# Layer 1's way out of attention: four K-tiles of the output weights converted during head 6, operand in two parts, sums begun between the last steps, last sums in small banks

## The chip, the core and the metric

The kernel runs on one core of a Trainium2 chip. The core has five engines with instruction streams of their own: TensorE (PE, matmuls and transposes; its weight loads are listed apart as PEld), VectorE (DVE), ScalarE (ACT), GpSimd (POOL) and SyncE (SP, which here only issues DMAs). An engine works through its stream in order and waits where an operand is not ready. Matmul results go into PSUM banks; all else lies in SBUF. The metric is device time of one launch in microseconds (us); lower is better.

## What is computed

Two layers over 512 latent tokens and 256 context tokens, width 1024, all in float32. Layer 1 is the one that matters here: eight heads of differential attention over all 768 keys, then an output projection, a gated residual, a norm and a SwiGLU block. Its context rows are needed as keys and values only, so its way out handles the 512 latent rows.

```python
def _diff_attend(q, k, v, lam):          # per head: two score maps
    s = einsum(q, k) * HEAD_DIM ** -0.5
    p = softmax(s)
    a = p[:, :, 0] - lam * p[:, :, 1]
    return einsum(a, v)
...
o = _rms(o, subln_w) * (1.0 - lam_init)          # per head
x = x + gx1 * (o.reshape(..., -1) @ w_out)       # way out of the mixer
x = x + gx2 * _swiglu(_rms(x, norm_ffn_w) * (1.0 + scx2) + shx2, ffn_w_in, ffn_w_out)
```

## The kernel before, in words

**Tiles.** Rows are taken in tiles of 128: latent tiles 0 to 3, context tiles 4 and 5. The contraction over the width runs in eight K-tiles of 128. Products keep float32 accuracy by splitting each operand into a high and a low part: three matmuls (hi·hi, hi·lo, lo·hi) per K-tile and per 512 output columns. A 1024 x 1024 product for one row tile is so 2 x 8 x 3 = 48 matmuls of 512 columns.

**Weights.** `unit` (L322) loads a raw tile by DMA on SP's queue, lets ACT cast it to the high part (L330) and lets DVE or POOL subtract to get the low part (L331). Raw tiles come from a ring of two (`raw_tile`), shared by all weights. `by_pieces` (L314) does the subtraction on POOL in pieces of 256 columns (L320). A high or low tile of a closed pool's place may be written once the tile that lay there is released.

**Layer 1.** For each head, `in_proj1` (L604) converts the head's weights with `by_pieces`, and then projects the six row tiles one by one (L428 to L430); each tile is normed and rotated (DVE, POOL), split, and transposed by the inner function `late()` (L647, L653), whose copies fill `qt` and `kT`. `attend1` (L659) is one step (head h, row tile t): scores into one of two wide PSUM slots (`p_sc`, L668 and L669), row maxima (L671), exponentials (L673), the difference of both maps (L680), then six transposes (`ppt`, L687), their copies (`PT`), the product with the values (`av`, L695), and a per-head norm (L697 to L702) that fills 128 columns of `o_t[t]`. `Staggered.push` puts the first half of a step ahead of the second half of the step before. All transposes take turns in two PSUM banks, `tr0` and `tr1` (`tr_tile`, L110): a new one waits until the tile two before it has been read.

**The way out of layer 1.** `OutProj` (L711): `weights` converts the eight K-tiles of `od_w_out`, `operand(t)` transposes `o_t[t]` into the room of the norm's output `hT` and splits it (L736 to L738), `sums(t)` makes both halves of 512 columns in one PSUM bank with a residual after each (L747 to L749, then L435 and L436), `last_sums` (L752) makes both halves at once in a wide slot. In the loop over head 7 (L1073 on), the weights begin at step 0, once the pools of the projection are closed (behind the marks of the last projected tile: `behind_marks`), K-tiles 0 to 3 in pool `w1u`, 4 to 7 in `w1d`. At steps 1 to 3 the loop adds `operand(t - 1)`, `sums(t - 1)` at a lower priority, and from step 2 the norm of tile t - 2. After the last step come `operand(3)`, the norm of tile 2, `last_sums(3)` and the norm of tile 3. The SwiGLU (`ffn`, L764) follows: for its first pair of hidden blocks it takes both wide slots and makes columns of rows 0 to 255 first (`first_segs`), then rows 256 to 511 (L791).

**Order.** The program is traced in the order of the source. A planner then lays out each engine's stream from priorities and its own model of time; the order on the chip is fixed. `tc.high_priority(-1000)` lowers the priority of what stands inside it, and `tc.issue_after(ins)` puts what stands inside it behind `ins` on the engine of `ins`. Turns in a tile ring follow the order of the source.

Of the kernel before, what the change touches and what calls it, by code (L numbers as in the profile page):

```python
# [63 lines left out]
def backbone(es: ExitStack, tc: tile.TileContext, x, c, ctx, c_ctx, mod_w, mod_b, norm_mix_w, norm_ffn_w,  # L64
# [50 lines left out]
    def f32(ap):  # L115
        return ap.bitcast(F32)
# [205 lines left out]
    def unit(pool, views, shape, bufs, name, sub=None, new_tile=raw_tile):  # L322

        raw = new_tile(shape, name + "r")
        for dst, src in views(raw):
            nc.sync.dma_start(dst, src)
        p_hi, p_lo = pool if isinstance(pool, tuple) else (pool, pool)
        hi = p_hi.tile(shape, F32R, name=name + "h", tag="whi", bufs=bufs)
        lo = p_lo.tile(shape, F32R, name=name + "l", tag="wlo", bufs=bufs)
        nc.scalar.copy(hi, raw)  # L330
        (sub or nc.vector.tensor_sub)(lo, raw, f32(hi))  # L331
        return hi, lo
# [271 lines left out]
    def in_proj1(h, tabs, wp, st, wh, qp):  # L604
# [14 lines left out]
        for t in CTX_FIRST:  # L619
# [35 lines left out]
            if t == CTX_FIRST[-1]:  # L655
                late()
# [48 lines left out]
    def out_units(wp, w_out, subs=(nc.gpsimd.tensor_sub,), rooms=(raw_tile,)):  # L705
        for k in range(KT):
            def views(raw, k=k):
                yield raw, w_out[0, k * P:(k + 1) * P, :]
            yield unit(wp[k // 4].pool, views, [P, D], 4, "wo", subs[k % len(subs)], rooms[k % len(rooms)])

    class OutProj:  # L711

        def __init__(self, l, units, o_t, xs, pool):
            self.l, self.units, self.ws, self.o_t, self.xs, self.g = l, units, [], o_t, xs, {}
            self.gates(2 if l == 0 else 1, pool, 0)
# [5 lines left out]
        def weights(self, n=KT):  # L721
            with behind_marks():
                self.ws.extend(w for _, w in zip(range(n), self.units))

        def operand(self, t):
            ohi, olo = tile_T(0, t), tile_T(1, t)
            if self.l == 0:
                self.xs[t] = load_x(t)
                nc.scalar.copy(ohi, self.o_t[t])
                nc.gpsimd.tensor_sub(olo, self.o_t[t], f32(ohi))  # L730
                return
            for q in range(2):
                pt = tr_tile("opt", [P, 4, P])
                for k in range(4):
                    kk = 4 * q + k
                    nc.tensor.transpose(pt[:, k, :], self.o_t[t][:, kk * P:(kk + 1) * P], ident)  # L736
                nc.scalar.copy(ohi[:, 4 * q:4 * q + 4], pt)
                nc.vector.tensor_sub(olo[:, 4 * q:4 * q + 4], pt, f32(ohi[:, 4 * q:4 * q + 4]))  # L738
            self.xs[t] = load_x(t, True)

        def sums(self, t, bank=None, pool=None, add=nc.vector):
            ohi, olo = tile_T(0, t), tile_T(1, t)
            for n in range(2):
                ps = acc_tile("ops", one=bank)
                for k in range(KT):
                    a, b = (z[:, n * 512:(n + 1) * 512] for z in self.ws[k])
                    nc.tensor.matmul(ps, ohi[:, k, :], a, start=k == 0, stop=False)  # L747
                    nc.tensor.matmul(ps, ohi[:, k, :], b, start=False, stop=False)  # L748
                    nc.tensor.matmul(ps, olo[:, k, :], a, start=False, stop=k == KT - 1)  # L749
                residual(self.xs[t], ps, self.g[0 if t < NTX else 1], n, pool, add, 1)  # L750
# [203 lines left out]
    for b in range(4):  # L954
# [9 lines left out]
        if b == 3:  # L964
# [7 lines left out]
            oproj = OutProj(0, out_units(ws, ev_w_out), o_t, xs, opa.pool)  # L972
# [72 lines left out]
    fp.close()  # L1045
    at = Pool("mix1")
# [60 lines left out]
    fp = Pool("ffn1")  # L1107
# [62 lines left out]
```

## Time and profile before

| | us |
|---|---|
| median of 3 runs | 1807.75 (1807.63 to 1808.97) |
| the profiled execution | 1810.42 |
| its span, first to last instruction | 1808.6 |
| mean granted TensorE clock | 0.985 |
| PE busy | 1725.4 (95%) |
| DVE, ACT, POOL busy | 1005.0, 809.2, 601.7 |
| last projection matmul of layer 1 begins | 1331.78 |
| first matmul of the way out begins | 1354.80 |
| first SwiGLU matmul of layer 1 begins | 1418.90 |
| first matmul of SwiGLU's second product begins | 1456.44 |

The page of the profile gives busy time per engine, a picture of the span in 40 slices with the granted clock, the chain that ended last and the costliest groups; its times count from the span's first instruction. Further views are the busy time by windows, the waits of an engine by the one that ended them, the groups by line and shape, and the timeline. In a windows row, "PE busy (xN)" is the time in which a matmul ran and the count of those that began; PEclk is 1.00 at full clock. In a group row the numbers after the bar are the summed busy time and the mean ns of one.

### The profile page before, as it was taken

The numbers are of one execution on the slowest core, as the hardware profiler recorded it, in microseconds if no ns is written. First come the engines' busy times: TensorE is split into PE (matmuls) and PEld (weight loads), VectorE is DVE, ScalarE is ACT, GpSimd is POOL, SyncE is SP. The second block draws the span as 40 slices with busy tenths as digits, with TensorE's granted clock in tenths as the row PEclk, the third lists the DMA queues.
The fourth block names the chain that finished last, engine by engine and source line by source line (L and its number), as shares of the span: only waits on it lengthen the run. The fifth ranks groups of instructions, "written<-read, shape, count | busy, mean of one in ns | idle before, by whom it ended". The sixth has DMA issues, their size and how long they took to land. (4 is left out here: it accounts for less than half of the span.)

```text
span 1808.6 us, 26168 instructions
## 1 busy us (share of the span) xinstructions
PE 1725.4 (95%) x9958; PEld 1462.3 (81%) x9958; DVE 1005.0 (56%) x1737; ACT 809.2 (45%) x1710; POOL 601.7 (33%) x866
## 2 busy tenths in 40 slices
PE   6999999989999999999999989999988899999998
PEld 3887776767888888888888889999986788888887
DVE  4776465444365555555543656665674455656553
ACT  6566555433354344344332566665663432222220
POOL 2753333321064344233312567776643100000000
PEclk8999999999999999999999999999989999999999
DMA  9212233213543234344421111111122233233231
GB/s 313 53 42 92 74 103 120 70 36 105 163 152 105 82 105 140 116 140 128 128 85 40 63 36 50 47 45 36 33 71 82 73 110 109 70 105 105 70 107 56
DMA packets 152477, 165.64 MB, mean 92 GB/s; under 512 B 16480, under 2 KB 139936, under 8 KB 152352
## 3 DMA queue, kind: packets, MB, share of 16 engines
q1 hardware_dynamic: 152000, 163.77, 28.7%
q8 instruction: 78, 1.28, 0.3%
q14 instruction: 47, 0.39, 0.1%
q10 hardware_dynamic: 352, 0.21, 0.0%
HBM read 159.73 MB, written 4.22 MB: 91 GB/s over the span
## 5 line engine op out<-in xcount | busy, mean ns | idle before, releaser
L435 DVE TENSOR_TENSOR dps<-dps,g 128x512 f32<-128x512 f32 x200 | 136.0, 695 | 108.5 <-PE dps L848 100.2
L846 PE MATMUL dps<-wdh,hdh 128*128 128x512 f32 x440 | 176.0, 401 | 0.9 <-DVE x L436 0.9
L847 PE MATMUL dps<-wdl,hdh 128*128 128x512 f32 x440 | 174.3, 396 | 0.0
L848 PE MATMUL dps<-wdh,hdl 128*128 128x512 f32 x440 | 168.1, 396 | 0.0
L428 PE MATMUL inps<-wih,hT 128*128 128x384 f32 x384 | 134.1, 349 | 2.3 <-ACT qkv L626 2.3
L436 DVE TENSOR_TENSOR x<-x,dps 128x512 f32<-128x512 f32 x200 | 131.9, 680 | 2.8
L429 PE MATMUL inps<-wil,hT 128*128 128x384 f32 x384 | 131.9, 343 | 0.0
L430 PE MATMUL inps<-wih,hT 128*128 128x384 f32 x384 | 131.4, 342 | 0.0
L791 PE MATMUL pg<-hT,wgh 128*128 128x512 f32 x352 | 129.8, 392 | 0.0
L791 PE MATMUL pu<-hT,wuh 128*128 128x512 f32 x352 | 129.4, 391 | 0.3 <-DVE x L436 0.3
L212 ACT ACTIVATE modw<-modw,cols 128x256 f32<-128x256 f32 x192 | 82.3, 498 | 81.7 <-DMA modw<-in_mod_w_dram 75.1
L791 PE MATMUL pgu<-hT,wgh 128*128 128x512 f32 (+1 forms) x384 | 114.2, 381 | 3.8 <-DVE x L436 2.9
L791 PE MATMUL pgu<-hT,wuh 128*128 128x512 f32 (+1 forms) x384 | 113.7, 376 | 0.0
L791 PE MATMUL pg<-hTc,wgh 128*128 128x256 f32 x352 | 98.7, 284 | 2.7 <-ACT hTc L307 2.4
L846 PEld LDWEIGHTS dps<-wdh,hdh 128*128 128x128 f32 x440 | 82.7, 188 | 22.5 <-issue 3.3
L791 PE MATMUL pu<-hTc,wuh 128*128 128x256 f32 x352 | 98.8, 285 | 0.0
L848 PEld LDWEIGHTS dps<-wdh,hdl 128*128 128x128 f32 x440 | 82.3, 188 | 19.7
L330 ACT CAST wgh<-wgr 128x1024 fp32r<-128x1024 f32 x44 | 46.1, 1049 | 116.0 <-PE pgu L791 69.5
L847 PEld LDWEIGHTS dps<-wdl,hdh 128*128 128x128 f32 x440 | 82.8, 188 | 17.9
L331 DVE TENSOR_TENSOR wgl<-wgr,wgh 128x1024 fp32r<-128x1024 f32 x44 | 54.3, 1236 | 75.5 <-ACT wgh L330 75.5
L320 POOL TENSOR_TENSOR wil<-wir,wih 128x256 fp32r<-128x256 f32 x96 | 76.4, 825 | 57.9 <-ACT wih L330 57.7
L331 DVE TENSOR_TENSOR wul<-wur,wuh 128x1024 fp32r<-128x1024 f32 x44 | 58.2, 1322 | 61.6 <-ACT wuh L330 61.6
(258 smaller groups left out, 4633.0 us busy)
## 6 DMA issues: line engine op xcount, KB each, us to landing
modw<-in_mod_w_dram SPq DMA_DIRECT2D x96, 512.0 KB, 4.5
wgr<-in_ffn_w_in_dram SPq DMA_DIRECT2D x44, 512.0 KB, 3.5
wur<-in_ffn_w_in_dram SPq DMA_DIRECT2D x44, 512.0 KB, 3.5
wdr<-in_ffn_w_out_dram SPq DMA_DIRECT2D x44, 512.0 KB, 3.6
wir<-in_od_w_in_dram SPq DMA_DIRECT2D x96, 128.0 KB, 2.3
x<-in_x_dram SPq DMA_DIRECT2D x8, 512.0 KB, 4.8
wir<-in_ev_w_in_dram SPq DMA_DIRECT2D x16, 256.0 KB, 2.9
wor<-in_ev_w_out_dram SPq DMA_DIRECT2D x8, 512.0 KB, 3.6
```

Of the source, the lines that this page charges most:

```text
L212: nc.scalar.activation(pr[:, k], w[:, k], AF.Copy, scale=cols[:, kk:kk + 1])
L320: nc.gpsimd.tensor_sub(lo[c], raw[c], hi[c])
L331: (sub or nc.vector.tensor_sub)(lo, raw, f32(hi))
L428: nc.tensor.matmul(ps, hs[0][:, k, :], a, start=k == 0, stop=False)
L429: nc.tensor.matmul(ps, hs[0][:, k, :], b, start=False, stop=False)
L430: nc.tensor.matmul(ps, hs[1][:, k, :], a, start=False, stop=k == KT - 1)
L435: nc.vector.tensor_mul(tmp, ps, g[:, n * 512:(n + 1) * 512])
L436: eng.tensor_add(xt[:, n * 512:(n + 1) * 512], xt[:, n * 512:(n + 1) * 512], tmp)
L791: nc.tensor.matmul(ps[:, s0:s1], a, cols_T(b, s0, s1)[:, k, :], start=k == 0 and q == 0, stop=k == KT - 1 and q == 2)
L846: nc.tensor.matmul(ps, hh, a, start=j == 0, stop=False)
L847: nc.tensor.matmul(ps, hh, b, start=False, stop=False)
L848: nc.tensor.matmul(ps, hl, a, start=False, stop=j == nj - 1)
```

## The change

Four things are moved, and each instruction keeps its size unless said.

- K-tiles 0 to 3 of `od_w_out` are converted in steps 1 and 2 of head 6, without the marks. Tiles 0 and 1 lie in a new pool `woe` (opened ahead of the attention's pool), 2 and 3 in the room of the context rows' `hTc`. Their subtractions go by pieces on POOL (16 pieces). K-tiles 4 to 7 are converted at step 0 of head 7, in `w1u`; their subtractions alternate between DVE and POOL.
- The operand of a tile is made in two parts: heads 0 to 6 (7 transposes) a step earlier, head 7 (1 transpose) when its step is done.
- The sums of tile 0, first half, begin in step 3 of head 6 with K-tiles 0 to 3 (12 matmuls), and `late()` of head 7's last projected tile is put behind them on PE; K-tiles 4 to 6 follow at step 0 of head 7, 7 at step 1; the second half at step 2. Tiles 1 to 3 are summed after the last step, with the norms between them.
- The last tile's sums use the two narrow banks, one for each half, and take K-tiles 4 to 7 first in the second half. The norms' rooms are in `opa`; `w1d` opens only for the SwiGLU.

```diff
-        p_hi, p_lo = pool if isinstance(pool, tuple) else (pool, pool)
-        hi = p_hi.tile(shape, F32R, name=name + "h", tag="whi", bufs=bufs)
-        lo = p_lo.tile(shape, F32R, name=name + "l", tag="wlo", bufs=bufs)
+        if callable(pool):
+            hi, lo = pool(shape)
+        else:
+            p_hi, p_lo = pool if isinstance(pool, tuple) else (pool, pool)
+            hi = p_hi.tile(shape, F32R, name=name + "h", tag="whi", bufs=bufs)
+            lo = p_lo.tile(shape, F32R, name=name + "l", tag="wlo", bufs=bufs)
...
             if t == CTX_FIRST[-1]:
+                if h == 7:
+                    yield
                 late()
...
-        def weights(self, n=KT):
-            with behind_marks():
+        def weights(self, n=KT, behind=True):
+            with behind_marks() if behind else ExitStack():
                 self.ws.extend(w for _, w in zip(range(n), self.units))
 
-        def operand(self, t):
+        def operand(self, t, k0=0, k1=KT):
             ohi, olo = tile_T(0, t), tile_T(1, t)
             if self.l == 0:
                 self.xs[t] = load_x(t)
                 nc.scalar.copy(ohi, self.o_t[t])
                 nc.gpsimd.tensor_sub(olo, self.o_t[t], f32(ohi))
                 return
-            for q in range(2):
-                pt = tr_tile("opt", [P, 4, P])
-                for k in range(4):
-                    kk = 4 * q + k
-                    nc.tensor.transpose(pt[:, k, :], self.o_t[t][:, kk * P:(kk + 1) * P], ident)
-                nc.scalar.copy(ohi[:, 4 * q:4 * q + 4], pt)
-                nc.vector.tensor_sub(olo[:, 4 * q:4 * q + 4], pt, f32(ohi[:, 4 * q:4 * q + 4]))
-            self.xs[t] = load_x(t, True)
-
-        def sums(self, t, bank=None, pool=None, add=nc.vector):
+            while k0 < k1:
+                m = min(4, k1 - k0)
+                pt = tr_tile("opt", [P, 4, P])[:, :m]
+                for k in range(m):
+                    nc.tensor.transpose(pt[:, k, :], self.o_t[t][:, (k0 + k) * P:(k0 + k + 1) * P], ident)
+                ks = slice(k0, k0 + m)
+                nc.scalar.copy(ohi[:, ks], pt)
+                nc.vector.tensor_sub(olo[:, ks], pt, f32(ohi[:, ks]))
+                k0 += m
+            if k1 == KT:
+                self.xs[t] = load_x(t, True)
+
+        def some(self, ps, t, n, ks, first, last):
             ohi, olo = tile_T(0, t), tile_T(1, t)
+            for k in ks:
+                a, b = (z[:, n * 512:(n + 1) * 512] for z in self.ws[k])
+                nc.tensor.matmul(ps, ohi[:, k, :], a, start=k == first, stop=False)
+                nc.tensor.matmul(ps, ohi[:, k, :], b, start=False, stop=False)
+                self.at = nc.tensor.matmul(ps, olo[:, k, :], a, start=False, stop=k == last)
+
+        def begin(self, t, n, bank, ks=range(KT)):
+            ps = acc_tile("ops", one=bank)
+            self.some(ps, t, n, ks, ks[0], None)
+            return ps
+
+        def end(self, ps, t, n, ks, pool=None, add=nc.vector):
+            self.some(ps, t, n, ks, None, ks[-1])
+            residual(self.xs[t], ps, self.g[0 if t < NTX else 1], n, pool, add, 1)
+
+        def sum(self, t, n, bank=None, pool=None, add=nc.vector, ks=range(KT)):
+            ps = acc_tile("ops", one=bank)
+            self.some(ps, t, n, ks, ks[0], ks[-1])
+            residual(self.xs[t], ps, self.g[0 if t < NTX else 1], n, pool, add, 1)
+
+        def sums(self, t, bank=None, pool=None, add=nc.vector, order=(range(KT), range(KT))):
             for n in range(2):
-                ps = acc_tile("ops", one=bank)
-                for k in range(KT):
-                    a, b = (z[:, n * 512:(n + 1) * 512] for z in self.ws[k])
-                    nc.tensor.matmul(ps, ohi[:, k, :], a, start=k == 0, stop=False)
-                    nc.tensor.matmul(ps, ohi[:, k, :], b, start=False, stop=False)
-                    nc.tensor.matmul(ps, olo[:, k, :], a, start=False, stop=k == KT - 1)
-                residual(self.xs[t], ps, self.g[0 if t < NTX else 1], n, pool, add, 1)
+                self.sum(t, n, bank, pool, add, order[n])
...
+    early = []
+
+    def in_ctx_room(shape):
+        if not early:
+            early.extend(ctx_room([P, 2, D], F32R, "woc"))
+        both = early.pop(0)
+        return both[:, 0], both[:, 1]
+
+    w1 = []
+
+    def out_pool(k):
+        return woe.pool if k < 2 else in_ctx_room if k < 4 else w1[0].pool
+
+    def late_raw(shape, name):
+        return opa.pool.tile(shape, F32, name=name, tag="wor", bufs=1)
+
+    def units1():
+        subs = (by_pieces, by_pieces, by_pieces, by_pieces, None, nc.gpsimd.tensor_sub, None, nc.gpsimd.tensor_sub)
+        for k in range(KT):
+            def views(raw, k=k):
+                yield raw, od_w_out[0, k * P:(k + 1) * P, :]
+            yield unit(out_pool(k), views, [P, D], 2 if k < 2 else 4, "wo", subs[k], late_raw if k == 6 else raw_tile)
+
+    oproj = OutProj(1, units1(), o_t, xs)
+
+    def norm1(t):
+        norm_hT(t, xs[t], 1, 1, opa.pool, tags=(("nh", 2), ("nhc", 2)))
+
     for h in range(8):
         for t in range(NTX):
             att.push(attend1(h, t, state[h], o_t, nlam, subln, at.pool))
+            if h == 6 and 1 <= t <= 2:
+                oproj.weights(2, False)
+            if h == 6 and t == 3:
+                oproj.operand(0, 0, 7)
+                ps = oproj.begin(0, 0, 0, range(4))
+                with tc.issue_after(oproj.at.ins):
+                    next(tiles)
             if h == 7 and t == 0:
                 wp.close()
                 whi.close()
@@ -1080,30 +1140,38 @@
                 tab.close()
                 states[2].close()
                 states[1].close()
-                w1 = [Pool("w1u", "right"), Pool("w1d", "right")]
+                w1.append(Pool("w1u", "right"))
                 opa = Pool("opa")
-                ws = out_units(w1, od_w_out, (nc.gpsimd.tensor_sub, None), (raw_tile, raw_tile, lambda shape, name:
-                               opa.pool.tile(shape, F32, name=name, tag="wor", bufs=1)))
-                oproj = OutProj(1, ws, o_t, xs, opa.pool)
                 oproj.weights()
-            if h == 7 and 0 < t <= 3:
-                oproj.operand(t - 1)
-
+                oproj.gates(1, opa.pool, 0)
                 with tc.high_priority(-1000):
-                    oproj.sums(t - 1, 0, opa.pool, nc.gpsimd)
-                if t == 2:
-                    room = ctx_room([P, 2, KT, P], F32, "nroom")
-                if t >= 2:
-                    norm_hT(t - 2, xs[t - 2], 1, 1, None, room=[z[:, t % 2] for z in room])
+                    oproj.some(ps, 0, 0, range(4, 7), None, None)
+            if h == 7 and t == 1:
+                oproj.operand(0, 7, KT)
+                oproj.operand(1, 0, 7)
+                with tc.high_priority(-1000):
+                    oproj.end(ps, 0, 0, [7], opa.pool, nc.gpsimd)
+            if h == 7 and t == 2:
+                oproj.operand(1, 7, KT)
+                oproj.operand(2, 0, 7)
+                with tc.high_priority(-1000):
+                    oproj.sum(0, 1, 0, opa.pool, nc.gpsimd)
             emit((h + 1) * NT + 2 + (2, 3, 5, 6)[t])
     att.flush()
+    oproj.operand(2, 7, KT)
     oproj.operand(3)
-    norm_hT(2, xs[2], 1, 1, None, room=[z[:, 0] for z in room])
-    oproj.last_sums(3)
-    norm_hT(3, xs[3], 1, 1, None, room=[z[:, 1] for z in room])
+    norm1(0)
+    oproj.sums(1, 0, opa.pool, nc.gpsimd)
+    norm1(1)
+    oproj.sums(2, 0, opa.pool, nc.gpsimd)
+    norm1(2)
+    oproj.sums(3, None, None, nc.vector, (range(KT), [4, 5, 6, 7, 0, 1, 2, 3]))
+    norm1(3)
     opa.close()
     states[0].close()
     at.close()
+    woe.close()
+    w1.append(Pool("w1d", "right"))
     fp = Pool("ffn1")
     ffn(1, xs, NTX, w1, fp.pool,
         lambda t, n: nc.sync.dma_start(out[0, t * P:(t + 1) * P, n * 512:(n + 1) * 512],
```

More of the change, by code (lines that the diff above doesn't have):

```diff
@@ L708, in views, with __init__ @@
                 yield raw, w_out[0, k * P:(k + 1) * P, :]
-            yield unit(wp[k // 4].pool, views, [P, D], 4, "wo", subs[k % len(subs)], rooms[k % len(rooms)])
+            yield unit(wp[k // 4], views, [P, D], 4, "wo", subs[k % len(subs)], rooms[k % len(rooms)])
     class OutProj:
-        def __init__(self, l, units, o_t, xs, pool):
+        def __init__(self, l, units, o_t, xs):
             self.l, self.units, self.ws, self.o_t, self.xs, self.g = l, units, [], o_t, xs, {}
-            self.gates(2 if l == 0 else 1, pool, 0)
         def gates(self, streams, pool, bank=None):
@@ L971, in backbone @@
             xs = [None] * NT
-            oproj = OutProj(0, out_units(ws, ev_w_out), o_t, xs, opa.pool)
+            oproj = OutProj(0, out_units([z.pool for z in ws], ev_w_out), o_t, xs)
+            oproj.gates(2, opa.pool, 0)
         for t in order:
@@ L1045, in backbone @@
     fp.close()
+    woe = Pool("woe")
     at = Pool("mix1")
```

## The prediction

> **What bounds the kernel now.** The page first: PE is busy nearly all the time, so a gain has to come from places where PE waits or runs at a lower clock.
>
> ```profile
> span 1808.6 us, 26168 instructions
> PE 1725.4 (95%) x9958; PEld 1462.3 (81%) x9958; DVE 1005.0 (56%) x1737; ACT 809.2 (45%) x1710; POOL 601.7 (33%) x866
> ```
>
> Then the busy time by windows, from the end of layer 1's last projection to SwiGLU's steady rhythm (1456.44, first matmul of its second product).
>
> ```profile
> core 0: us, PE busy (x) PEld busy (x) DVE busy (x) ACT busy (x) POOL busy (x), PEclk, DMA share, GB/s
> 1333.87:1339.15 5.28, 1.54 (x13) 1.06 (x11) 1.56 (x4) 4.00 (x10) 4.27 (x7) 0.93 0.34 101
> 1339.15:1348.50 9.35, 8.39 (x33) 7.20 (x33) 6.97 (x9) 5.01 (x11) 2.29 (x2) 0.50 0.30 112
> 1348.50:1366.61 18.11, 12.97 (x90) 11.21 (x88) 14.66 (x23) 13.35 (x29) 6.70 (x9) 0.97 0.52 172
> 1366.61:1373.30 6.69, 6.69 (x21) 5.19 (x21) 4.28 (x5) 1.13 (x2) 2.36 (x1) 0.56 0.47 144
> 1373.30:1413.23 39.93, 37.63 (x190) 29.70 (x189) 12.70 (x24) 12.99 (x31) 12.04 (x17) 1.00 0.05 17
> 1413.23:1434.11 20.88, 18.01 (x107) 15.60 (x106) 14.71 (x20) 10.59 (x16) 4.58 (x5) 1.00 0.43 136
> 1434.11:1437.40 3.29, 3.29 (x15) 3.29 (x16) 0.00 (x0) 1.12 (x2) 1.86 (x3) 0.50 0.28 97
> 1437.40:1456.44 19.04, 16.89 (x140) 16.29 (x139) 6.80 (x11) 8.24 (x12) 0.00 (x0) 1.00 0.16 56
> sum 122.57, PE 105.41 PEld 89.55 DVE 61.67 ACT 56.43 POOL 34.11; mean PE 13.18 PEld 11.19 DVE 7.71 ACT 7.05 POOL 4.26
> ```
>
> PE stands still for 122.57 - 105.41 = 17.2 us. The clock takes more: of 8.39 us at 0.50, 6.69 at 0.56 and 3.29 at 0.50, full clock would save 4.2, 2.9 and 1.6, together 8.7. So 26 of these 122.6 us are not work. PE's waits name the causes (total, times, longest):
>
> ```profile
> PE ops L747 <- ACT hT L737: 4.3, 3, 3.2
> PE pgu L791 <- DVE x L436: 2.9, 1, 2.9
> PE qpt L647 <- ACT qd L634: 2.4, 1, 2.4
> PE ops L748 <- POOL wol L331: 1.9, 1, 1.9
> PE sc L668 <- ACT e L673: 1.0, 1, 1.0
> PE ppt L687 <- ACT kT L654: 0.9, 1, 0.9
> PE ops L747 <- DVE rtmp L435: 0.7, 1, 0.7
> ```
>
> After the three longest the clock is halved; the 1.9 kept it. A wait of some 2.4 us costs about twice itself here, a shorter one only itself.
>
> **The change part by part.** PE's work stays: 192 matmuls of the way out, 32 operand transposes, 32 for norms. What can change is waits, clock and order.
>
> *Begun sums.* PE has nothing to do while the last tile is rotated and split. The change puts 12 matmuls and 7 transposes there. Their prices, from two matmuls of an unbroken run and one row of 8 transposes:
>
> ```profile
> 1387.01 0.40 PE L748 MATMUL ops<-wol,hT 128*128 128x512 f32 x1
> 1392.15 0.39 PE L749 MATMUL ops<-woh,hT 128*128 128x512 f32 x1
> 1441.06 1.03 PE L298 MATMUL npt<-cst,nroom 128*128 128x128 f32 x8
> ```
>
> 22 steps in 5.14 us are 0.234 each: 12 take 2.8, and 7 transposes 0.9. That is 3.7 us against 5.28 - 1.54 = 3.7 of standstill. The first two windows lost 3.7 + 1.0 + 4.2 = 8.9. The chain to `kT` itself is not shortened, and `late()` now stands behind the 12 matmuls. I keep the waits for `kT` (0.9) and `e` (1.0) and 0.6 for the new queue, and no halved clock, since no piece is near 2.4. Gain **6.4**; bounds 2 (filled too late, the clock still falls) and 8.9.
>
> *K-tiles 0 to 3 out of head 7.* Eight casts and eight subtractions stand among the steps and ahead of the first sums:
>
> ```profile
> 1338.87 2.54 DVE L331 TENSOR_TENSOR wol<-wor,woh 128x1024 fp32r<-128x1024 f32 x1 [1.06 <-ACT woh L330]
> 1364.08 1.99 ACT L330 CAST woh<-wor 128x1024 fp32r<-128x1024 f32 x2 [0.15 <-DMA wor<-in_od_w_out_dram]
> 1365.98 0.58 ACT L737 CAST hT<-opt 128x512 fp32r<-128x512 f32 x1
> 1367.53 2.52 DVE L331 TENSOR_TENSOR wol<-wor,woh 128x1024 fp32r<-128x1024 f32 x1 [0.19 <-ACT woh L330]
> ```
>
> The chain that ended last prices a DMA, a cast and a subtraction on POOL:
>
> ```profile
> 1352.01 4.97 DMA wor<-in_od_w_out_dram
> 1357.00 1.06 ACT woh L330
> 1358.12 2.36 POOL wol L331
> ```
>
> The operand's copy stood behind two casts (the 3.2 us wait), and the last low part came at 1370. With four K-tiles left, two raw tiles can be loaded before head 7; the last is due at 1341.4 (the first subtraction's end frees a raw place) + 5.0 + 1.1 + 2.4 = 1350. Windows three and four lost 5.1 us standing and 2.9 by clock, 8.0. Late next is the ring of transposes: the operand's part for head 7 waits for the norm of step (7, t), and the next step's `ppt` comes behind it. I leave 1.4. Gain **6.6**; bounds 2.5 and 8.0.
>
> *Norms behind the last step.* A step's `ppt` stood in the ring behind an earlier tile's norm:
>
> ```profile
> 1356.67 1.02 DVE L680 SCALAR_TENSOR_TENSOR e<-e,rt 128x768 f32<-128x768 f32 x1
> 1392.38 0.82 PE L687 MATMUL ppt<-cst,e 128*128 128x128 f32 x6
> ```
>
> Step (7, 2) was ready at 1357.7 and transposed at 1392.4. This goes, but gains little: sums filled the time (37.63 of 39.93). After, steps end early and the sums of tiles 1 to 3 (144 matmuls, 33.7 us) follow; three turns of the one bank cost up to 0.7 each (the wait for `rtmp`), with norm transposes to fill them. Old loss 2.3, new the same: **0**; bounds -2.8 and 2.3.
>
> *Small banks for the last sums.* The last sums hold a wide slot until their residual is through; SwiGLU needs both, hence the 2.9 us wait and a halved clock. That goes. The last tile's norm must then hide behind the columns of rows 0 to 255: 96 matmuls of 256, by half the rhythm 11.2 us. Its chain before, from the `x` it waits for:
>
> ```profile
> 1434.09 1.06 ACT L290 ACTIVATE nroom<-x 128x1024 f32<-128x1024 f32 x1 [3.34 <-DVE x L436]
> 1436.24 1.12 POOL L292 TENSOR_SCALAR nroom<-x,rs_n 128x1024 f32<-128x1024 f32 x1
> 1444.51 1.29 DVE L308 TENSOR_TENSOR hT<-nroom,hT 128x512 fp32r<-128x512 f32 x2 [0.33 <-ACT hT L307]
> ```
>
> That is 11.7 us, of which PE's order took 3.7 (1437.36 to 1441.06): 8.0 bare, with a residual ahead and four casts beside it 11 to 13. SwiGLU's first weights wait for the places of K-tiles 4 to 7, free from 4.9 us (21 matmuls) before the end; a cast and a subtraction need less. Lost here were 2.9 + 2.1 (last window) + 1.6 = 6.6; I leave 2.1. Gain **4.5**; bounds 0 and 6.6.
>
> *Head 6 pays.* Four casts on ACT and 16 pieces on POOL:
>
> ```profile
> L320 POOL TENSOR_TENSOR wil<-wir,wih 128x256 fp32r<-128x256 f32 x96 | 76.4, 825 | 57.9 <-ACT wih L330 57.7
> 1280.00:1300.00 20.00, 18.73 (x137) 17.56 (x136) 15.01 (x29) 13.34 (x35) 16.06 (x27) 1.00 0.23 73
> 1300.00:1333.87 33.87, 33.87 (x238) 32.90 (x236) 22.95 (x49) 21.14 (x56) 15.24 (x31) 1.00 0.06 17
> ```
>
> 16 x 0.825 = 13.2: POOL goes from 15.2 to 28.4 of 33.9 us. Behind a piece on POOL wait the power, `qy` and `kd` of a projected tile and the norm of a step; behind these PE's transposes. The nearest row is head 7's own conversion, 12 pieces about 1280 to 1300: PE lost 1.27 us at POOL 80%. For 16: 1.7. On ACT 4 x 1.06 come to 21.1, still the less busy engine. The DMAs cost nothing: raw places are free once head 7's own weights are converted, SP has nothing to issue between this row and the loads of `x` at 1318, and the DMA share in head 6 is 0.06:
>
> ```profile
> 1290.88 4.94 SPq L326 DMA_DIRECT2D wor<-in_od_w_out_dram  x2
> ```
>
> The gate's row and the loads of `x` keep their steps of head 7, where only K-tiles 6 and 7 are still to be loaded; without that cover a DMA's 5.0 us would stand ahead of the first residual, behind which only bank 0 waits. Cost **-1.7**; bounds -6.6 (each piece holds PE for half its length) and 0.
>
> Pool `woe` also shifts the attention's room, whose first tiles then wait for other tiles of layer 0. No row prices it; I take nothing, within 2 us both ways.
>
> Sum: 6.4 + 6.6 + 0 + 4.5 - 1.7 = **15.8 us**. The profiled execution (1810.42, span 1808.6) would become 1794.6; it was 2.67 above the median of 1807.75, which would become **1792.0**.
>
> **The rivals.** *All filled* (0.11): the upper ends but head 6, 8.9 + 8.0 + 6.6 - 1.7 = 21.8: 1786.0. For it: whole sums are at hand after 1350; against: the new queue in the ring.
>
> *A new chain of steps* (0.21): the single transpose makes each step wait for the norm of the one before, so waits move instead of going: 2 + 2.5 + 4.5 - 1.7 = 7.3: 1800.5. For it: 35 us between (7, 2)'s two rows show how the ring holds a step; against: a step's own norm is far shorter than sums and a tile's norm.
>
> *Pieces hold DVE* (0.12): each piece keeps DVE, and so PE, for half its length: 6.4 + 6.6 + 4.5 - 6.6 = 10.9: 1796.9. For it: a low part on DVE took 2.54 us at 1338.87; against: PE was full in head 6 and has work in hand. The Trainium skill, "SBUF — State Buffer", section "SBUF: two separate sides", says that VectorE with two SBUF inputs and GpSimd share one port pair as an exclusive lock, the later one waiting for the other's whole instruction; this rule gives this rival's time.
>
> *It doesn't do what it says* (0.06): the planner leaves the pieces until after the last projection. The begun sums then stand ahead of `late()` and wait for the last low part: four pieces, 3.3 us, eat most of the small banks' 4.5: 1806.5, the same.
>
> *Slower* (0.06): the pieces give PE waits of 2.4 us in head 6, and the clock is halved there. Each piece holding PE its whole length, 13.2, and half of 33.9 us at half clock, 17: 30.2 against the other terms' 17.5: 1820.4. It decides where a piece costs PE over 17.5 / 16 = 1.1 us. Against it: 12 pieces cost 0.1 each.
>
> **How the numbers follow.** The forecast has 0.44. The terms' distances to their bounds, added as squares, are 5 us towards faster and 9.6 towards slower, and the outer half of the latter is the rivals': its own range is 1787 to 1797; to leave out no more than 2 in 10 it must reach both partial cases: **1785 to 1802**. A measurement can tell 0.2%, 3.6 us, from no change: faster 0.88, same 0.06, slower 0.06.
>
> **What would show it.** Begun sums right: `ops` matmuls between the last projection and `late()`'s transposes, clock 1.00 to the first scores. Conversion right: four `wol` before the last projection matmul, the last of all near 1350. Steps right: `ppt` of (7, 3) soon after its `e`. Small banks right: no wait of `pgu` for `x`. Head 6 wrong: PE busy under 32 of its 34 us, or a clock below 1.00. The prediction is wrong if standstill and lost clock from the last projection to the second product stay above 16 us, or if head 6 loses over 5.

## The result and the profile after

| | before | after |
|---|---|---|
| median (4 runs each) | 1808.36 us (1807.63 to 1809.37) | 1793.97 us (1790.93 to 1796.07) |
| ratio, 95% interval | | 0.9919 (0.9902 to 0.9936) |
| the profiled execution, its span | 1810.42, 1808.6 | 1790.93, 1789.1 |

The change takes 14.6 us (0.0081 of 1808), and 1792.0 had been predicted. The size is right; the reasons are not, as the runs below show.

The head of the page after, and the busy time by windows from head 7's first projection matmul to the first matmul of SwiGLU's second product:

```profile
span 1789.1 us, 26195 instructions
PE 1718.5 (96%) x9958; PEld 1455.3 (81%) x9958; DVE 998.0 (56%) x1738; ACT 807.0 (45%) x1713; POOL 608.9 (34%) x880
```

```profile
core 0: us, PE busy (x) PEld busy (x) DVE busy (x) ACT busy (x) POOL busy (x), PEclk, DMA share, GB/s
1279.13:1318.61 39.48, 36.37 (x243) 33.95 (x242) 21.70 (x48) 23.90 (x59) 30.17 (x56) 1.00 0.33 100
1318.61:1333.39 14.78, 11.28 (x85) 9.45 (x85) 10.60 (x21) 11.62 (x30) 10.12 (x15) 1.00 0.33 92
1333.39:1338.82 5.43, 5.43 (x29) 4.20 (x29) 0.93 (x2) 0.86 (x2) 0.38 (x1) 1.00 0.12 42
1338.82:1357.41 18.59, 14.19 (x90) 10.97 (x87) 16.36 (x29) 13.70 (x30) 4.09 (x5) 1.00 0.34 113
1357.41:1377.87 20.46, 17.05 (x79) 13.75 (x79) 4.36 (x9) 4.11 (x10) 5.89 (x7) 0.92 0.09 27
1377.87:1411.17 33.30, 33.11 (x166) 27.31 (x166) 15.23 (x26) 11.71 (x25) 10.36 (x14) 1.00 0.02 6
1411.17:1437.06 25.89, 24.78 (x210) 24.36 (x209) 15.21 (x24) 15.67 (x26) 2.92 (x3) 1.00 0.46 145
```

Read by itself this looks as forecast: the begun sums (third row) run at full clock, the last row has no wait for `x`, and the second product begins at 1437.06 instead of 1456.44. But the first row already begins at 1279.13, where the kernel before had 1291.03. So 11.9 of those 19.4 us were won before the way out begins, far from anything that the prediction priced.

For the runs below except e5, e6, e10 and e12, five instants of the profiled execution. "Exit" is the last column less the first. The last `av` is the row of PE's timeline in which the last step's products with the values begin: all 12 matmuls of the step, in e8 only the last four (the other eight begin at 1387.55).

| kernel | head 7's projection begins | its last matmul | last `av` begins | SwiGLU begins | its second product begins | exit |
|---|---|---|---|---|---|---|
| before | 1291.03 | 1331.78 | 1410.30 | 1418.90 | 1456.44 | 165.4 |
| after | 1279.13 | 1318.61 | 1389.03 | 1411.17 | 1437.06 | 157.9 |
| e1, place only | 1283.66 | 1324.72 | 1403.38 | 1411.97 | 1448.86 | 165.2 |
| e2, no shift | 1289.38 | 1328.82 | 1396.76 | 1418.95 | 1444.95 | 155.6 |
| e3, small banks only | 1294.08 | 1334.91 | 1412.54 | 1421.38 | 1457.77 | 163.7 |
| e4, head 7's part later | 1279.06 | 1318.55 | 1372.74 | 1407.00 | 1431.33 | 152.3 |
| e7, wide last sums | 1281.26 | 1320.46 | 1390.72 | 1412.81 | 1442.48 | 161.2 |
| e8, norms last and small banks | 1292.45 | 1333.14 | 1400.54 | 1420.79 | 1449.50 | 157.1 |
| e11, no begun sums | 1280.37 | 1319.81 | 1372.07 | 1406.51 | 1430.84 | 150.5 |
| e13, three places for `qkv` | 1285.30 | 1325.84 | 1402.47 | 1411.07 | 1448.23 | 162.9 |

One profile is one run, up to 3.5 us off its kernel's median in these rows: the instants show where the time lies, the ratios how much it is. 0.001 of a ratio is 1.8 us.

### The profile page after: what moved, and what is told of

It reads as the page before. It is cut to its first block, busy times and chain, and to the rows that moved or that the text cites. A ratio compares the mean times of both kernels' runs of the same rounds, so it can differ in the third digit from the quotient of the medians.

```text
span 1789.1 us, 26195 instructions
## 1 busy us (share of the span) xinstructions
PE 1718.5 (96%) x9958; PEld 1455.3 (81%) x9958; DVE 998.0 (56%) x1738; ACT 807.0 (45%) x1713; POOL 608.9 (34%) x880
## 4 chain that ended last, share of the span: by engine, by line
PE 71%; issue 6%; POOL 6%; ACT 4%; DVE 4%; DMA 4%; SPq 1%; ACTq 0%; POOLq 0%; DVEq 0%
PE pgu L813 13%; PE pu L813 8%; PE pg L813 8%; PE dps L868 5%; PE dps L869 5%; PE dps L870 5%; PE inps L431 3%; PE inps L432 3%; PE inps L433 3%; POOL wil L320 2%; PE av L582 2%; PE sc L537 2%; PE ops L752 2%; PE ops L754 2%; PE ops L753 2%
```

## The experiments

### Where the early 12 us come from

**e1: the kernel before, with the attention's room shifted as the change shifts it.**

```diff
+    opa = Pool("opa")
+    opa.pool.tile([P, 1536], F32, name="place")
     at = Pool("mix1")
...
-                opa = Pool("opa")
```

> The kernel before, with its pool `opa` opened ahead of the attention's pool and filled to 16 KB; nothing else of the change. All tiles of the attention then lie where the change puts them, and the way out is the old one. Theory (the place): in the two traces 11.9 of the 19.4 us are there before head 7's projection begins, because head 0's `vv` no longer lies over the last norm's `nhc`; so 9 to 12 us faster than before (ratio 0.9934 to 0.9950), head 7's first projection matmul near 1279 instead of 1291, and the stretch from there to the first matmul of SwiGLU's second product as long as before, 165 us. Rival (the way out is what gained, and the earlier start is chance of one profile): no change, ratio 1.000 within 0.001.

Measured: 1800.74 us, ratio 0.9958 (0.9944 to 0.9973), 7.6 us faster (4.9 to 10.1). In its profile the exit is as long as before (165.2 against 165.4), and all of the gain lies at layer 1's start. Busy time by windows there, before:

```profile
1024.00:1032.00 8.00, 3.75 (x28) 3.26 (x26) 4.51 (x10) 5.10 (x13) 0.53 (x2) 0.95 0.00 0
1032.00:1068.00 36.00, 30.81 (x164) 28.75 (x165) 15.31 (x36) 18.18 (x43) 24.15 (x43) 0.82 0.16 45
```

and in e1:

```profile
1024.00:1032.00 8.00, 8.00 (x54) 7.92 (x53) 5.67 (x16) 4.07 (x11) 5.14 (x11) 1.00 0.00 0
1032.00:1068.00 36.00, 31.73 (x185) 29.23 (x185) 17.61 (x39) 21.49 (x53) 23.86 (x42) 0.91 0.20 60
```

From 1024 to 1068 PE ran 191 matmuls before and 238 with the shift: it no longer stands for half of 1024 to 1032, and the clock lies at 0.91 instead of 0.82 behind it. The theory of the place holds; its size came out somewhat below the 9 to 12 expected from two single profiles.

**e2: the kernel after without the shift** (pool `woe` between the states, so that the attention's tiles lie as before).

```diff
-    woe = Pool("woe")
     at = Pool("mix1")
...
-    states = [Pool(f"state{i}") for i in range(3)]
+    states = [Pool("state0"), Pool("state1")]
+    woe = Pool("woe")
+    states.append(Pool("state2"))
```

> The kernel after, with pool `woe` opened between the second and the third pool of head states, so that the attention's tiles and the states of heads 0 and 1 lie where they lay before; K-tile 6's raw tile takes the ring of two, as room for a third is short. Theory (the place): the early gain is lost and that of the way out stays: 1800 to 1803, ratio 0.9955 to 0.9975 to before; `vv` waits for `nhc` again until about 1031. Rival (the way out gained): ratio 0.992 as after, 1794.

Measured: 1802.36 us, ratio 0.9965 (0.9953 to 0.9977). The way out alone is worth 6.3 us (4.2 to 8.5). Place and way out add up: 7.6 + 6.3 = 13.9 against 14.6 for both.

**e6: is it the one overlap?** Before, POOL's first copy into head 0's `vv` waited 7.64 us for layer 0's last norm, whose `nhc` lies under the end of that tile. Here layer 0's tiles lie 768 bytes further up, clear of `vv`.

```diff
     fp = Pool("ffn0")
+    fp.pool.tile([P, 192], F32, name="place")
```

> The kernel before with a tile of 768 bytes at the head of the pool of layer 0's SwiGLU: its tiles lie 768 bytes further up, and head 0's `vv`, which lay over the lowest 640 bytes of `nhc`, lies clear of it by 128 bytes; all else keeps its neighbours. Theory (that one overlap): the same 9 to 12 us as the full shift, first copy into `vv` near 1012 instead of 1031. Rival (the other tiles of the attention count: `e`, `PT`, `qt`, `kT` over the norm's and the modulation's tiles): under 3 us.

Measured: 1806.71 us, ratio 0.9999 (0.9987 to 1.0010): no gain. The timeline of e6 tells why:

```profile
1023.30 0.52 POOL L627 COPY vv<-qkv 128x128 f32<-128x128 f32 x2
...
1030.56 0.50 ACT L626 COPY qkv<-inps 128x384 f32<-128x384 f32 x1
```

The wait is gone and the copy into `vv` comes 7.8 us earlier, but the planner still put it behind other work of POOL. ACT's third copy into `qkv`, which needs the place that this copy frees, still stands behind the last norm. So it is not enough to clear that one overlap, and the theory that it alone cost 9 to 12 us is refuted. What the next run tests is the place that the copy holds up.

**e13: the kernel before, with three places for `qkv`.** No tile of the attention moves.

```diff
-            raw = wp.tile([P, 384], F32, name="qkv", tag="qkv", bufs=2)
+            raw = wp.tile([P, 384], F32, name="qkv", tag="qkv", bufs=3)
```

> The kernel before with a ring of three for the projected tiles (`qkv`) in place of two. Theory (the place counts since `vv` of head 0 comes free late, its copies hold the ring of two, and the third projected tile of layer 1 then stands behind the last norm in ACT's order): with a third place the projection goes on, 4 to 9 us of the early gain without any shift, ratio 0.995 to 0.998. Rival (the ring is not what holds the order at layer 1's start): ratio above 0.999, the third copy still near 1031.

Measured: 1802.29 us, ratio 0.9959 (0.9946 to 0.9973), the same as the shift. The timeline before:

```profile
1031.14 0.53 POOL L627 COPY vv<-qkv 128x128 f32<-128x128 f32 x2 [7.64 <-DVE hT L308]
1031.46 0.48 ACT L626 COPY qkv<-inps 128x384 f32<-128x384 f32 x1 [0.65 <-POOL vv L627]
...
1031.99 0.69 PE L428 MATMUL inps<-wih,hT 128*128 128x384 f32 x1 [2.27 <-ACT qkv L626]
```

and of e13, the third copy into `qkv` and the group of its first five copies into `vv`:

```profile
1022.12 0.48 ACT L626 COPY qkv<-inps 128x384 f32<-128x384 f32 x1 [1.12 <-PE inps L430]
...
L627 POOL COPY vv<-qkv x5: 293/297/551, 1034.4 to 1036.7; 128x128 f32<-128x128 f32 x5
```

Before, three rows in a chain: `vv` waits for the norm, `qkv` for `vv`, PE for `qkv`. In e13 `vv` is still written only from 1034.4, behind the norm, but the third projected tile leaves its bank at 1022.12 and PE goes on: it is busy for 8.00 us of 1024 to 1032, against 3.75 before and 4.25 in e6. So it is shown that the ring of two held the projection. That the late room of `vv` held the ring is read from the three rows above; e6 adds that the planner's order held it as well, and why the planner kept that order without the overlap is open. In the kernel after the first copy into `vv` runs at 1012.76 and the third copy into `qkv` at 1018.56.

### What the way out is worth, part by part

**e3: the kernel before with the small banks alone.**

```diff
-    oproj.last_sums(3)
+    oproj.sums(3)
```

> The kernel before with only the last tile's sums in the two narrow banks. By the traces the stretch from the last sums to the first matmul of SwiGLU's second product lost 7.3 us before and 1.6 after, so 4.5 (the prediction's term) to 5.7 us faster: ratio 0.9968 to 0.9975, with no wait of `pgu` for `x` and no halved clock there. Rival (the last tile's norm then comes late for rows 256 to 511, or SwiGLU's weights do): under 2 us, ratio above 0.9989, with a new wait of PE on `hT` or on SwiGLU's weights.

Measured: 1808.18 us, ratio 1.0004 (0.9994 to 1.0013): nothing. The wait of `pgu` for `x` (2.87 us before) went, and one of `npt` for the last tile's norm came, here in the timeline of PE. The third row's wait was there before too, with 1.26 us. The clock still halves, only later: 0.58 from 1444.90 to 1447.50.

```profile
1421.35 0.27 PE L736 MATMUL opt<-cst,o 128*128 128x128 f32 x1
...
1440.81 1.09 PE L298 MATMUL npt<-cst,nroom 128*128 128x128 f32 x8 [1.22 <-POOL nroom L292]
...
1443.40 0.28 PE L251 MATMUL gps<-cst,modc 128*8 128x128 f32 x1 [1.50 <-ACT nroom L303]
```

The last tile's operand is only complete at 1421.35, because step (7, 3) ends late (last `av` 1412.54). Its sums then run among SwiGLU's first columns, and SwiGLU's other columns wait for its norm.

**e8: norms of tiles 0 and 1 behind the last step, and the small banks.**

```diff
-                if t == 2:
-                    room = ctx_room([P, 2, KT, P], F32, "nroom")
-                if t >= 2:
-                    norm_hT(t - 2, xs[t - 2], 1, 1, None, room=[z[:, t % 2] for z in room])
...
-    norm_hT(2, xs[2], 1, 1, None, room=[z[:, 0] for z in room])
-    oproj.last_sums(3)
+    room = ctx_room([P, 2, KT, P], F32, "nroom")
+    for t in range(3):
+        norm_hT(t, xs[t], 1, 1, None, room=[z[:, t % 2] for z in room])
+    oproj.sums(3)
```

> The kernel before with the norms of tiles 0 and 1 moved behind the last step and the last tile's sums in the narrow banks; weights, operands and sums of tiles 0 to 2 as before. Theory (a step of head 7 that stands in the ring of transposes behind an earlier tile's norm makes the last tile's operand late, and the small banks pay only without that): 3 to 6 us faster than before, ratio 0.9967 to 0.9983, the last `av` before 1395 instead of 1413 and a tail without the wait for the norm's chain. Rival (the gain of the tail hangs on sums left for the end, which this kernel doesn't have): within 1.5 us, ratio above 0.9992.

Measured: 1801.18 us, ratio 0.9973 (0.9961 to 0.9985), 4.9 us faster (2.7 to 7.0). The last `av` begins at 1400.54 instead of 1410.30, later than the 1395 expected, and the exit shrinks by 8.3 us in the profile. The tail is not free of the norm's chain, as had been expected: `pgu` still waits 2.69 us for `hT` there. With the norms behind the last step the two edits give what the small banks alone did not. The norms' move with the wide sums was not run on the kernel before, so how the 4.9 us divide between the two is not shown.

**e7: the kernel after with the wide last sums.**

```diff
-    oproj.sums(3, None, None, nc.vector, (range(KT), [4, 5, 6, 7, 0, 1, 2, 3]))
+    oproj.last_sums(3)
```

> The kernel after with the last tile's sums in a wide slot again, as before. The small banks alone gave nothing, yet the stretch around SwiGLU's first blocks lost 1.6 us with the whole change against 7.4 before. Theory (the banks count once the last tile's sums start without waiting for its operand): 3 to 6 us slower than after, ratio 0.9935 to 0.995, with a wait of `pgu` for `x` of about 3 us and a halved clock. Rival (the tail's gain comes from the new order alone): as after, 0.992 within 0.001.

Measured: 1796.50 us, ratio 0.9938 (0.9920 to 0.9955): 3.4 us over after's ratio, though the intervals overlap, so that the banks' worth in this order is likely but not shown. The wait that comes in is not the one expected; in its timeline PE stands for the norm's chain, and behind it the clock does halve (0.50 from 1418.40 to 1420.60):

```profile
1418.44 1.11 PE L298 MATMUL npt<-cst,nh 128*128 128x128 f32 x4 [3.53 <-ACT nhc L303]
```

**e10: place, norms last and small banks on the kernel before** (the edits of e1 and e8 together). Early weights, split operand and begun sums are left out, and the sums of tiles 0 to 2 stay between the steps.

> The kernel before with the shift of the attention's room, the norms of tiles 0 and 1 behind the last step and the narrow banks: the place and the new tail, without the four early K-tiles, the operand in two parts and the begun sums. Theory (these two parts are the whole gain of the change, and what it does during head 6 and head 7 is given back there): the parts add up to 7.6 + 4.9 = 12.5 us, ratio 0.9925 to 0.9935, within 2 us of after. Rival (early weights and begun sums are worth the 4 us or more of the prediction): 1798 or more, ratio above 0.9945.

Measured: 1794.05 us, ratio 0.9920 (0.9903 to 0.9937), against 0.9919 for the whole change. (Its profiled run took 1801.6, 7.5 over its median, so its instants are not in the table.) The parts that were meant as the core of the change, priced at 6.4 + 6.6 - 1.7 = 11.3 us, add nothing that can be measured; the two intervals leave some 4 us either way.

### Where the gain of the early weights went

**e4: the kernel after with head 7's part of the operand one step later.** Only the place in the order changes: `operand(0, 7, KT)` and the last K-tile's sums go from step 1 to step 2, `operand(1, 7, KT)` and the second half's sums from step 2 to step 3.

```diff
             if h == 7 and t == 1:
-                oproj.operand(0, 7, KT)
                 oproj.operand(1, 0, 7)
+            if h == 7 and t == 2:
+                oproj.operand(0, 7, KT)
+                oproj.operand(2, 0, 7)
                 with tc.high_priority(-1000):
                     oproj.end(ps, 0, 0, [7], opa.pool, nc.gpsimd)
-            if h == 7 and t == 2:
+            if h == 7 and t == 3:
                 oproj.operand(1, 7, KT)
-                oproj.operand(2, 0, 7)
```

> The kernel after with head 7's single transpose of a tile's operand (and the sums that need it) one step later, so that a step's transposes no longer stand in the ring behind the norm of the step just before. Theory (the ring is what eats the gain of the K-tiles: the steps and sums of 1339 to 1378 still lost 12 us in the profile of after): 3 to 5 us faster than after, ratio 0.9885 to 0.990 to before, the waits of `ppt` for `hT` gone. Rival (the steps are held by their own chains of scores, exponentials and copies): as after, 0.992 within 0.001.

Measured: 1784.39 us, ratio 0.9873 (0.9857 to 0.9890): the fastest kernel here, 8.3 us below after by the ratios (5.7 by the exits of the two profiles), more than the 3 to 5 expected; the two intervals leave some 4 us either way. PE's timeline of after, steps (7, 1) to (7, 3):

```profile
1352.01 0.66 PE L692 MATMUL ppt<-cst,e 128*128 128x128 f32 x4 [0.17 <-DVE hT L743]
1354.24 0.33 PE L740 MATMUL opt<-cst,o 128*128 128x128 f32 x1 [1.57 <-DVE o L707]
...
1363.11 0.38 PE L692 MATMUL ppt<-cst,e 128*128 128x128 f32 x2
...
1371.55 0.66 PE L692 MATMUL ppt<-cst,e 128*128 128x128 f32 x4 [1.42 <-DVE hT L743]
...
1372.88 2.07 PE L700 MATMUL av<-vv,PT 128*128 128x128 f32 x8 [0.57 <-ACT PT L697]
```

and of e4:

```profile
1352.89 0.66 PE L692 MATMUL ppt<-cst,e 128*128 128x128 f32 x4 [0.17 <-DVE hT L743]
1355.89 0.30 PE L740 MATMUL opt<-cst,o 128*128 128x128 f32 x1 [0.52 <-DVE o L707]
...
1358.95 0.66 PE L692 MATMUL ppt<-cst,e 128*128 128x128 f32 x4 [0.63 <-DVE hT L743]
...
1365.40 0.38 PE L692 MATMUL ppt<-cst,e 128*128 128x128 f32 x2
1366.86 0.82 PE L692 MATMUL ppt<-cst,e 128*128 128x128 f32 x6
...
1372.74 1.50 PE L700 MATMUL av<-vv,PT 128*128 128x128 f32 x12
```

In after the single `opt` (tile 0's part for head 7) waits 1.57 us for the norm of step (7, 0), and the second half of step (7, 1)'s transposes stands behind it in the ring. They come so late that (7, 2) begins its own at 1371.55, where its first eight `av` take 2.07 us instead of 1.16 at half clock, and the last `av` of (7, 3) begins at 1389.03. In e4 (7, 2) begins at 1358.95 and the last step's `av` at 1372.74, 16.3 us earlier, and dense sums follow. From 1330 to there PE's waits for `opt` fall from 1.6 to 0.5 us, those of the sums for `rtmp` from 2.4 to nothing; those of `ppt` for `hT`, which had been expected to go, fall from 1.6 to 0.8. The order of e4 was not tried without the early K-tiles, so how much of its gain is theirs is not shown.

**e5: the kernel after with the conversions behind the marks.** Its trigger was that after's planner drew the 16 pieces forward to between 1285 and 1301, where POOL is full and PE falls behind.

```diff
-                oproj.weights(2, False)
+                oproj.weights(2)
```

> The kernel after with the conversions of K-tiles 0 to 3 put behind the marks of the projection, as all other weights are. Theory (the planner drew the 16 pieces on POOL forward to 1283 to 1301, where they push head 6's steps behind the last projection, so 10 us are still lost around its end): 2 to 4 us faster than after, ratio 0.990 to 0.991. Rival (they are then late, and the begun sums wait for the low parts): 1 to 4 us slower than after, ratio 0.9925 to 0.994.

Measured: 1791.69 us, ratio 0.9917 (0.9902 to 0.9932): as after. The windows of e5 show both halves of it:

```profile
1290.00:1300.00 10.00, 10.00 (x70) 9.61 (x69) 6.52 (x14) 5.56 (x16) 3.34 (x8) 1.00 0.01 2
...
1328.00:1332.20 4.20, 0.00 (x0) 0.00 (x0) 1.12 (x2) 2.13 (x6) 3.86 (x8) 0.78 0.50 168
1332.20:1337.00 4.80, 4.59 (x10) 3.20 (x11) 1.64 (x4) 1.08 (x2) 3.19 (x3) 0.50 0.55 175
```

The projection keeps PE full, but the begun sums wait 4.3 us for an operand's copy behind K-tile 4's cast on ACT, and then run at half clock. That is neither of the two expectations: what one place gains the other loses.

**e12: e4 with the conversions at steps 0 and 1, behind the marks.**

```diff
-            if h == 6 and 1 <= t <= 2:
-                oproj.weights(2, False)
+            if h == 6 and t <= 1:
+                oproj.weights(2)
```

> The kernel of the later head 7 part with the conversions of K-tiles 0 to 3 at steps 0 and 1 of head 6, behind the marks of the projection. Theory (drawn forward to 1283 to 1301 the 16 pieces cost 3 us of the projection, and at steps 1 and 2 behind the marks they came too late for the begun sums, which waited 4.3 us for a copy of the operand; between the two both costs go): 2 to 4 us faster, ratio 0.985 to 0.9865. Rival (POOL's 13 us have to stand somewhere in head 6 and head 6's steps are late anyway): ratio 0.987 to 0.9885.

Measured: 1791.42 us, ratio 0.9892 (0.9875 to 0.9910): 3.4 us over e4's ratio with overlapping intervals. It is not the gain that the theory expected, and the number lies just above the rival's. In its profile the projection takes 40.7 us instead of 39.5, and from its end to the last `av` it is 55.3 instead of 54.2. Whether it is slower at all is not settled, nor which wait would do it.

**e11: e4 without the begun sums.** Tile 0's first sums start at step 0 of head 7 with seven K-tiles, and `late()` of the last projected tile waits for nothing new.

```diff
-                ps = oproj.begin(0, 0, 0, range(4))
-                with tc.issue_after(oproj.at.ins):
-                    next(tiles)
...
-                    oproj.some(ps, 0, 0, range(4, 7), None, None)
+                    ps = oproj.begin(0, 0, 0, range(7))
```

> The kernel of the later head 7 part with no sums before head 7's first step: all seven K-tiles of tile 0's first half are summed at step 0 of head 7, and the last projected tile's transposes wait for nothing new; the early conversions and the split operand stay. Theory (the begun sums are worth what the prediction gave them where the clock would fall, 4.2, and the standstill, some 2): 4 to 6 us slower than with them, ratio 0.9895 to 0.9905, the clock at half at the first scores of head 7. Rival (the standstill there is filled by head 6's late steps in any case): within 1.5 us of it, ratio 0.9865 to 0.988.

Measured: 1787.19 us, ratio 0.9872 (0.9857 to 0.9887), as e4's 0.9873. Windows of e11 behind the last projection:

```profile
1325.00:1330.00 5.00, 3.44 (x28) 2.79 (x26) 4.14 (x8) 5.00 (x13) 3.22 (x5) 1.00 0.04 17
1330.00:1335.00 5.00, 4.00 (x28) 3.41 (x29) 2.42 (x4) 3.69 (x11) 2.98 (x3) 1.00 0.61 182
1335.00:1340.00 5.00, 5.00 (x31) 4.23 (x30) 4.51 (x8) 3.54 (x10) 1.44 (x2) 1.00 0.10 33
```

Without a begun sum PE is busy for 12.4 of 15 us and keeps its clock: head 6's late steps fill the place. In after, e4 and e11 the `av` of eight steps follow the last projection, in the kernel before and in e5 those of seven.

## Why the prediction was right, and where it was wrong

The time came out at 1793.97 for 1792.0 by luck: the way out was priced at 15.8 and gave 6.3 (e2), the place at nothing and gave 7.6 (e1). By its own steps:

| step | predicted | measured |
|---|---|---|
| begun sums | 6.4 | 0, within some 4 (e11 against e4) |
| K-tiles 0 to 3 out of head 7 | 6.6 | 0 within some 4, together with begun sums and split operand (e10 against after); the order of e4 adds 8.3 |
| norms behind the last step | 0 | 4.9 with the small banks (e8) |
| small banks | 4.5 | 0 alone (e3) |
| head 6 pays | -1.7 | in the row of the K-tiles, not apart |
| shift of the attention's room | 0, within 2 | 7.6 (e1), 7.4 by way of the ring (e13) |

- **"Pool `woe` also shifts the attention's room ... No row prices it; I take nothing, within 2 us both ways."** This is the step that failed most. There was a row, in the timeline of before shown at e13: a copy into `vv` waiting 7.64 us for layer 0's norm, with PE standing 2.27 us behind it, and the clock at 0.82 from 1032 to 1068. The prediction looked at the end of layer 1 only, and at what the new tiles wait for, not at what the old places had been waiting for. e1, e2 and e13 show the gain from three sides.
- **"Begun sums ... Gain 6.4."** The rows of before were read rightly; the standstill was there. But the same change puts 16 pieces on POOL, one more of head 6's steps slips behind the projection, and these steps fill it. e11 shows that then the sums add nothing that can be measured. It was tried on e4's order, not on the kernel before.
- **"Late next is the ring of transposes ... I leave 1.4. Gain 6.6."** The mechanism was named and its price too small: e4, which shifts the single transpose one step back in the ring, gains 8.3. The rival *a new chain of steps*, given 0.21, is what the way out did: it had 7.3 us for the way out, and e2 measured 6.3 (4.2 to 8.5). Whether the early K-tiles are worth their 6.6 once the ring is out of the way is not shown.
- **"Old loss 2.3, new the same: 0" and "Small banks ... Gain 4.5".** The two are one term. The last tile is late because step (7, 3) ends late, and the small banks alone are worth nothing while that holds (e3). With the norms moved the two gave 4.9 where 4.5 had been counted for the banks; the norms' own share is not told apart.
- **"Head 6 pays ... -1.7."** PE stands for 39.48 - 36.37 = 3.1 us of head 7's projection, where the kernel before had 1.27 standing from 1280 to 1333.87. The standstill has the size that was forecast; what it costs in time is not shown, since e5 took it away and was as fast as after. Nor do the reasons hold. "The DMAs cost nothing" was wrong: three of the early casts wait 0.65 to 0.85 us for their loads. PE's two waits beside the pieces (0.66 and 0.91 us) end on ACT's copies into `qkv`, the second of them like this:

```profile
1295.79 1.05 ACT L333 CAST woc<-wor 128x1024 fp32r<-128x1024 f32 x1 [0.65 <-DMA wor<-in_od_w_out_dram]
1296.74 0.47 ACT L629 COPY qkv<-inps 128x384 f32<-128x384 f32 x1
...
1297.27 0.44 PE L431 MATMUL inps<-wih,hT 128*128 128x384 f32 x1 [0.91 <-ACT qkv L629]
```

  The rival *pieces hold DVE* had 6.6 us for head 6. The trace shows no such cost: the three VectorE instructions with two inputs in SBUF that ran, at least in part, beside the 16 pieces took 1.02 us (`e`, 1284.33), 0.29 (`qy`, 1286.58) and 0.43 (`qd`, 1289.21), no longer than clear of any piece. Beside K-tile 7's subtraction on POOL (2.63 us from 1347.90) a step's `e` did take 2.09 us instead of 1.01. The Trainium skill, "SBUF — State Buffer", section "SBUF: two separate sides", says that a VectorE instruction with two inputs in SBUF and a GpSimd one that reads SBUF exclude each other. The subtraction's case fits that rule; beside the pieces no wait by it is seen.
- **What was to show it.** One mark failed, and rightly, and one stood on its edge. *Steps right: `ppt` of (7, 3) soon after its `e`* stands in after's timelines of DVE and PE like this:

```profile
1357.28 1.01 DVE L685 SCALAR_TENSOR_TENSOR e<-e,rt 128x768 f32<-128x768 f32 x1
...
1374.75 1.06 PE L692 MATMUL ppt<-cst,e 128*128 128x128 f32 x4
```

  16.5 us lie between the end of the one and the start of the other. The mark for head 6, PE busy under 32 of its 34 us, was met or missed by the choice of the window: 31.34 of the 33.87 us up to the last projection matmul, 32.00 with the window 2.1 us later, placed as the prediction's row was. The other marks came out as for a right prediction: `ops` ahead of `late()` at full clock, the last low part done at 1347.9 + 2.63 = 1350.5, no wait for `x`, and from the last projection to the second product 118.45 - 105.84 = 12.6 us of standstill and 17.05 x 0.08 = 1.4 by the clock, 14.0 under the mark of 16. That last one was too weak: standstill and clock fell by 12 in that stretch, but it became only 6.2 us shorter (118.45 against 124.66), because work had moved into it from ahead. A length between two fixed instants would have told.

## What to carry to other kernels

When a change opens a pool below others, list which tiles then lie over which older ones, and follow each old wait to the engine at its end: here a copy that nobody needed soon held a ring of two, the ring held a projection, and a third place of 1.5 KB gave 7.4 us without any of the rest. Where two edits touch the same late event, such as the end of the last step, price them as one term, and undo them singly and together. To judge a stretch compare two fixed instants, not its idle time, since idle time also falls when work is pushed into it.

## What the runs showed of the hardware

The prediction took a single wait of about 2.4 us as what halves the clock. In after two waits of 1.42 and 0.57 us with short transposes between were enough. Windows of after around the rows shown for e4's comparison:

```profile
1369.30:1371.50 2.20, 0.83 (x7) 0.52 (x5) 0.70 (x2) 1.24 (x4) 0.74 (x2) 1.00 0.00 0
1371.50:1372.80 1.30, 0.77 (x5) 0.53 (x5) 0.25 (x1) 0.56 (x2) 0.00 (x0) 1.00 0.04 13
1372.80:1374.70 1.90, 1.82 (x8) 1.82 (x9) 0.29 (x1) 0.20 (x2) 0.00 (x0) 0.50 0.62 147
1374.70:1376.30 1.60, 1.60 (x8) 1.46 (x7) 0.00 (x0) 0.00 (x0) 0.00 (x0) 0.53 0.38 154
```

PE was busy for 0.83 + 0.77 = 1.60 of the first 3.5 us, and the next 3.5 ran at half. How much work in such a stretch keeps the clock was not measured.

The same kernel also spreads more than its first runs told: 28 runs of before beside e1, e2, e3 and e6 on one chip went from 1803.62 to 1812.78 us, 0.5%, where the first four had lain within 0.1%.
